# Moving the split tokens' rows by 128 bytes, and another first batch of idle matmuls

## The chip, the core and the metric

The kernel runs on one core of one Trainium2 chip. The metric is the device time of one execution in microseconds (us). Five engines work side by side, each through its own instruction queue in order: TensorE (PE in the profile; its weight loads are a row of their own, PEld), VectorE (DVE), ScalarE (ACT), GpSimd (POOL) and SyncE (SP). Here SP and POOL start nearly all transfers (DMA), and ACT starts the first five.

## The reference, cut to what matters

One layer of a decoder trunk is computed for 4096 prompt tokens and 64 sample tokens, all in float32:

```
h = rmsnorm(x) * norm_pre
z = h @ w_in                    # 1024 -> 2816 columns: the input projection
out_a = silu(g) * B * conv3(C * h_in)
out_b = silu(g) * window_attention(q, k, v, sinks)
out_c = silu(g) * cross_attention(q, memory)
y = concat(out_a, out_b, out_c) @ w_out
x = x + rmsnorm(y) * norm_post
```

The projection `z` is 22 column tiles of 128 for 4160 tokens; with `y` it is most of the arithmetic.

## The kernel before, in words

**How a product is made.** TensorE multiplies float32 at full speed only in the rounded type `float32r`. So each operand is split into a rounded part `hi` and a remainder `lo`, and a product is three matmuls: `hi` of the weights with `hi` of the tokens, `hi` with `lo`, and `lo` with `hi`. `product` (L360 to L368) does this for one weight tile of 512 rows by 128 columns and one tile of 260 tokens: 4 slices of 128 rows by 3 matmuls, 12 matmuls of 260 columns, all at L367. Each has its own weight load. The token rows (`hi`, `lo`) are the moving operand, which streams through the array; the weight slices are the stationary operand, which is loaded into it.

**The input projection.** Token blocks of 520 (two tiles of 260) and weight tiles in pairs go through Strassen-Winograd products (seven instead of eight); the first two blocks go through eight plain products. `PHASES` lists the pairs of column tiles in three phases. A phase's weights stay in SBUF while all eight blocks pass. Altogether L367 is executed 7488 times: 624 products of 12.

**Where the operands lie.** Tiles come from pools that are laid out one behind the other in every partition. The weight slots (`wa`, `wb`; 4096 bytes each) begin at byte 224 of a 256-byte period in both pools; a slice lies 512 bytes behind the one before it, so all weight slices begin at 224 modulo 256. `split` (L354) and `x_split` (L576) put `hi` and `lo` into slots of pool `hp`, tiles of 4 rows of 320 floats (1280 bytes, five periods; 260 floats are used). In the kernel before, `hp` begins so that every such row lies at 96 modulo 256: 128 bytes off the weights. These residues are read from the addresses in the built program.

**The output projection** (`Block.run`, L1491) swaps the roles: the weights of `w_out` (in slots of `wa`) are the moving operand with 512 columns, and the split rows `mh`, `ml` of 128 tokens (also in slots of `wa`) are the stationary one, so both lie at 224 modulo 256. One block is an exception: the 64 sample tokens' rows `mh_s` lie in another pool's tile at 96. The last block also has matmuls of 256 columns, from the same slots.

**The start.** POOL fills `ident`, `mhalf` and `ones`; ACT and SP load the first tokens and weights. Meanwhile TensorE runs nine idle matmuls (L701, `ones` times `ident`, float32, whose records are 18 of 128 columns), whose result is not used. The first products then wait for the first weights, split by ACT (L181) and DVE (L185).

**What sets the order.** The program up to the end of phase 0 is kept in the written order on all engines (`manual_schedule`, opened just ahead of the first loads); the rest is ordered by a scheduler. The change moves no instruction in it.

Of the kernel before, what the change touches and what calls it, by code (L numbers as in the profile page):

```python
# [8 lines left out]
F32 = mybir.dt.float32  # L9
F32R = mybir.dt.float32r  # L10
# [5 lines left out]
P = 128  # L16
D = 1024
KT = D // P
KH = KT // 2
# [5 lines left out]
XR = 320  # L25
# [22 lines left out]
def f(ap):  # L48
    return ap.bitcast(F32)
# [3 lines left out]
def hybrid_layer(ctx: ExitStack, tc: tile.TileContext, a: dict):  # L53
    nc = tc.nc
    TE, V, S, G, DMA = nc.tensor, nc.vector, nc.scalar, nc.gpsimd, nc.sync
# [7 lines left out]
    ident = const.tile([P, P], F32, name="ident")  # L63
# [21 lines left out]
    pa = ExitStack()  # L85
# [3 lines left out]

    place = ctx.enter_context(tc.tile_pool(name="place", bufs=1)).tile([P, 2, KH, HW], F32, name="place")  # L90
    hxp = pa.enter_context(tc.tile_pool(name="hx", bufs=4))
    hp = pa.enter_context(tc.tile_pool(name="hp", bufs=2))
    own = ExitStack()
    kept_z = ExitStack()
# [38 lines left out]
    def accumulator(i, w, name):  # L133

        tag = "xy"[i % 2]
        if pa1 is None:
            return pa2[tag].tile([P, 2, 512], F32, tag=tag, name=name)
        return pa1[tag, w].tile([P, w, 512], F32, tag="c", name=name)
# [367 lines left out]
    ones = own.enter_context(tc.tile_pool(name="ones", bufs=1)).tile([P, P], F32, name="ones")  # L506
# [69 lines left out]
    def x_split(b, o, meanwhile=lambda: None):  # L576
        x = xs[0, b][o]
        h0[b, o] = hi, lo = [hp.tile([P, KH, XR], F32R, tag=n, name=f"{n}0_{b}{o}")[:, :, :HW] for n in ("hi", "lo")]
        for k in range(KH):
            if k == 1:  # L580
                meanwhile()
            g = gain_of(o, k)
            S.mul(hi[:, k], x[:, k], g)
            V.scalar_tensor_tensor(lo[:, k], x[:, k], g, f(hi[:, k]), op0=ALU.mult, op1=ALU.subtract)
# [5 lines left out]
    def first_fill(o, q, raw=None):  # L590
        ws[0, q, o] = w_slot(q, f"w0_{q}{o}")
        w_split(ws[0, q, o], raw0.pop((q, o)) if raw is None else raw)
# [104 lines left out]
    x_of(0, 0, "B21")  # L697

    idle = accumulator(1, 2, "idle")
    for _ in range(9):  # L700
        TE.matmul(idle[:, 0, :P], ones, ident, start=True, stop=True)  # L701
    x_split(0, "B11", lambda: first_fill("A21", 0))
    for q in range(4):
        if q > 0:
# [977 lines left out]
```

## Time and profile before

| | us |
|---|---|
| median of 3 runs | 1545.25 |
| lowest and highest | 1545.03, 1546.0 |
| span of the profiled execution | 1545.6 |
| TensorE busy in it | 1535.3 |
| VectorE busy | 1145.3 |
| ScalarE busy | 805.6 |
| GpSimd busy | 378.5 |
| PE line L367 on the chain that ended last | 48.9% of the span |

The span runs from the first to the last instruction of one profiled execution; it is 0.35 us above the median of the runs. Times inside the execution are counted from the span's start. In rows of the timeline the columns are: start, time from the first start to the last end (us), engine, line, operation, output and inputs, size, count, and in brackets the engine's idle time just ahead and what ended it. Matmuls are pipelined: one of 260 columns is recorded with about 0.28 us, while the next one starts about 0.12 us after it. So the pace of a stretch is the time from one start to a later start, divided by the number of matmuls between them.

### The profile page before, as it was taken

The page shows a single profiled execution, that of the slowest core. Times are in us where ns is not written, and L with a number is a line of the kernel's source. Part 1 is how long each engine was busy: PE and PEld are TensorE (multiplying, and loading weights), DVE is VectorE, ACT ScalarE, POOL GpSimd, SP SyncE. Part 2 cuts the span into 40 slices and gives each one's busy share as a digit, 9 for nine tenths or more (in the row PEclk, how much of TensorE's full clock was granted, in tenths as well). Part 3 has the DMA queues.
Part 4 walks back from the last instruction along what each step waited for, and adds up shares of the span by engine and source line. Part 5 has one row for each costly group of instructions (what it writes and reads, how often), then busy time and mean ns, then how long its engine had stood idle before and what let it go on. Part 6 is the DMA issues. An engine that isn't in the chain of part 4 may idle for free.

```text
span 1545.6 us, 30168 instructions
## 1 busy us (share of the span) xinstructions
PE 1535.3 (99%) x11341; PEld 1413.2 (91%) x11341; DVE 1145.3 (74%) x2055; ACT 805.6 (52%) x2039; POOL 378.5 (24%) x603
## 2 busy tenths in 40 slices
PE   9999999999999999999999999999999999999998
PEld 9999999999999999999999998788888888887876
DVE  6779887898888777896777769766666666666643
ACT  6776665475322222344454447665556655655632
POOL 0223332211400000000100203544444444444310
PEclk9999999999999999999999999999999999999999
DMA  9879999778755333578777788987777677777432
GB/s 282 187 203 234 272 281 268 264 241 299 193 180 179 126 125 113 196 221 278 229 259 244 207 303 264 243 159 164 147 159 149 147 151 161 150 161 154 129 110 95
DMA packets 177942, 306.28 MB, mean 198 GB/s; under 512 B 33925, under 2 KB 107653, under 8 KB 177765
## 3 DMA queue, kind: packets, MB, share of 16 engines
q1 hardware_dynamic: 130901, 227.38, 47.4%
q0 software_dynamic: 46176, 75.92, 24.9%
q8 instruction: 90, 1.47, 0.4%
q10 hardware_dynamic: 720, 1.05, 0.2%
q14 instruction: 55, 0.45, 0.1%
HBM read 197.23 MB, written 108.05 MB: 198 GB/s over the span
## 4 chain that ended last, share of the span: by engine, by line
PE 87%; DMA 5%; DVE 4%; issue 2%; POOL 1%; ACT 1%; SPq 0%; ACTq 0%; DVEq 0%; POOLq 0%
PE c L367 49%; PE y L1491 22%; PE ws L1245 4%; PE wo L1087 2%; PE wt L1268 2%; PE xs L1181 2%; PE xt L1196 2%; PE wo L1217 2%; DMA md<-th 1%; PE wo L1223 1%; DVE z L374 1%; PE mem_acc L788 1%; DMA qd<-z 1%; DMA nat<-in_x_p 1%; DMA x_4B<-in_xt 1%
## 5 line engine op out<-in xcount | busy, mean ns | idle before, releaser
L1491 PE MATMUL y<-wo,mh 128*128 128x512 f32 (+1 forms) x1040 | 350.1, 399 | 0.0
L374 DVE TENSOR_TENSOR z<-c,z 128x520 f32<-128x520 f32 (+1 forms) x308 | 194.8, 646 | 90.1 <-PE c L367 89.0
L1491 PEld LDWEIGHTS y<-wo,mh 128*128 128x128 f32 x1040 | 194.3, 188 | 39.4 <-issue 2.4
L1491 PE MATMUL y<-wo,ml 128*128 128x512 f32 (+1 forms) x520 | 201.9, 388 | 0.0
L1258 ACT ACTIVATE sm<-sm,wnm 128x128 f32<-128x128 f32 x256 | 99.6, 391 | 60.8 <-DVE wnm L1252 60.0
L1190 POOL TENSOR_SCALAR xp<-xp,xrd 128x256 f32<-128x256 f32 x128 | 74.3, 588 | 208.1 <-DVE xrd L1186 208.1
L1491 PEld LDWEIGHTS y<-wo,ml 128*128 128x128 f32 x520 | 98.2, 189 | 16.2
L1182 DVE TENSOR_REDUCE xmx<-xs 128x2 f32<-128x512 f32 x64 | 44.1, 689 | 59.6 <-PE xs L1181 59.3
L1270 ACT COPY wpt<-wt 128x512 f32<-128x512 f32 x64 | 37.3, 582 | 86.8 <-PE wt L1268 84.3
L1245 PEld LDWEIGHTS ws<-kst,q 128*128 128x128 f32 x512 | 70.1, 190 | 5.4 <-ACT xp L1185 0.7
L1498 DVE TENSOR_TENSOR yn<-y,gpost 128x512 f32<-128x512 f32 (+1 forms) x66 | 45.1, 683 | 39.6 <-PE y L1491 39.3
L1245 PE MATMUL ws<-kst,q 128*128 128x256 f32 x512 | 73.1, 283 | 0.4 <-ACT xp L1185 0.4
L1499 ACT ACTIVATE y<-y 128x512 f32<-128x512 f32 (+1 forms) x66 | 38.6, 584 | 64.2 <-DVE yn L1498 64.2
L736 POOL CAST wmask<-negs 128x256 uint8<-128x256 f32 x1 | 1.1, 1076 | 270.9 <-DMA negs<-in_wmask 270.9
L1278 POOL TENSOR_SCALAR_AFFINE_SELECT wpt<-wpt 128x512 f32<-128x512 f32 x64 | 52.6, 821 | 42.7 <-ACT wpt L1270 39.8
L1185 ACT ACTIVATE xp<-xs,xnm 128x256 f32<-128x256 f32 x128 | 58.9, 464 | 7.1 <-DVE xnm L1183 7.1
L1120 POOL DMA_DIRECT2D q<-qd x64 | 42.8, 674 | 71.2 <-DVE wo L185 61.1
L1109 POOL DMA_DIRECT2D kst<-qd x64 | 38.7, 617 | 63.9 <-PE xt L1196 41.5
L1248 DVE COPY_PREDICATED sm<-wmask,ws 128x256 f32<-128x256 uint8 x124 | 52.2, 436 | 2.7 <-ACT sm L1247 2.3
L1509 DVE SCALAR_TENSOR_TENSOR xr<-yn,yst,xr 128x1024 f32<-128x1024 f32 (+2 forms) x34 | 43.1, 1269 | 14.2 <-POOL yst L1505 13.3
L376 ACT COPY z<-c 128x520 f32<-128x520 f32 (+1 forms) x44 | 24.3, 553 | 55.8 <-PE c L367 53.3
L1275 POOL TENSOR_SCALAR_AFFINE_SELECT wpv<-wpt 128x512 f32<-128x512 f32 x62 | 40.2, 648 | 50.8 <-ACT wpt L1270 50.7
(961 smaller groups left out, 5144.1 us busy)
## 6 DMA issues: line engine op xcount, KB each, us to landing
q<-qd POOLq DMA_DIRECT2D x64, 384.0 KB
xr<-in_x_p SPq DMA_DIRECT2D x32, 512.0 KB
nat<-in_x_p SPq DMA_DIRECT2D x39, 416.0 KB
o_yp<-xr SPq DMA_DIRECT2D x31, 512.0 KB
md<-th POOLq DMA_DIRECT2D x48, 260.0 KB
qd<-zh SPq DMA_DIRECT2D x48, 260.0 KB
qd<-z SPq DMA_DIRECT2D x48, 260.0 KB
kst<-qd POOLq DMA_DIRECT2D x60, 192.0 KB
```

Of the source, the lines that this page charges most:

```text
L367: TE.matmul(bank[:, :HW], l, r, start=first and i == 0, stop=last and i == 3 * KH - 1)
L374: add = lambda dst, other: V.tensor_tensor(dst, c, other, op=ALU.add)
L1182: V.tensor_reduce(mx[:, :nb], s, axis=AX.X, op=ALU.max)
L1185: S.activation(p[:, i, :], s[:, i, :], AF.Exp, bias=nm[:, i : i + 1], scale=SCALE, accum_out=den[:, i : i + 1])
L1190: G.tensor_scalar(p[:, i, :], p[:, i, :], rd[:, i : i + 1], 0.5, op0=ALU.mult, op1=ALU.mult)
L1245: TE.matmul(s3[:, hh, :], self.q[:, 4 + 2 * (2 * half + hh) + kvh, i * P : i * P + P], self.kst[:, 2 * kvh + part, i * P : i * P + 2 * P], ...
L1248: V.copy_predicated(sm[:, 2 * half : 2 * half + 2, :], third["wmask"], third["negs"] if first else s3[:, :, 0:P])
L1258: S.activation(sm[:, hh, :], sm[:, hh, :], AF.Exp, bias=nm[:, hh : hh + 1], scale=SCALE, accum_out=den[:, hh : hh + 1])
L1278: G.affine_select(p3, p3, pattern=[[0, 4], [1, P]], compare_op=ALU.is_ge, fill=0.0, base=0, channel_multiplier=-1)
L1491: TE.matmul(acc, self.hl[l][:, k], wo[k][c0 // 512][:, r, c0 % 512 : c0 % 512 + c1 - c0], start=j == 0, stop=j == passes * KT - 1)
L1498: V.tensor_tensor(yn[:m, c0:c1], acc[:m], gpost[:m, c0:c1], op=ALU.mult)
L1509: V.scalar_tensor_tensor(self.xr[:m, cs], yn[:m, cs], st[:m, 3:4], self.xr[:m, cs], op0=ALU.mult, op1=ALU.add)
```

## The change

A pool `shift` of 32 floats (128 bytes) is put between the pools `hx` and `hp`, and never written or read. It moves `hp`, and the pools laid out behind it for the projection (row factors, temporaries, `z` tiles), by 128 bytes. Every row of `hi` and `lo` then lies at 224 modulo 256, like the weights. The pools of the output projection and the attention keep their addresses, since they are opened anew once the projection's pools are closed.

The nine idle matmuls of 128 columns give way to fourteen of 260 to 512 columns (5488 in all), on a tile of ones in the rounded type, which takes a slot of `hp` and is filled by POOL.

```
+    pa.enter_context(tc.tile_pool(name="shift", bufs=1)).tile([P, 32], F32, name="shift")
     hp = pa.enter_context(tc.tile_pool(name="hp", bufs=2))
...
     idle = accumulator(1, 2, "idle")
-    for _ in range(9):
-        TE.matmul(idle[:, 0, :P], ones, ident, start=True, stop=True)
+    warm = hp.tile([P, KH, XR], F32R, tag="lo", name="warm").rearrange("p k n -> p (k n)")
+    G.memset(f(warm[:, : P + 512]), 1.0)
+    for n in (416, 416, 416, 416, 512, 512, 512, 416, 416, 416, 260, 260, 260, 260):
+        TE.matmul(idle[:, 0, :n], warm[:, :P], warm[:, P : P + n], start=True, stop=True)
```

Three lines more stand ahead of the rest, so L367 becomes L368 and L701 becomes L704.

The first rows of TensorE's queue at the start of the program, before (`idle` is the unused result, `c` an accumulator of the projection, `hi`, `lo` the split tokens, `w` the split weights):

```order
L701 MATMUL idle<-ident,ones 128x128 x9
L367 MATMUL c_0_0_0_267<-hi_0B_229,w_0A_233 128x260
L367 MATMUL c_0_0_0_267<-lo_0B_230,w_0A_233 128x260
L367 MATMUL c_0_0_0_267<-hi_0B_229,w_0A_233 128x260 x2
L367 MATMUL c_0_0_0_267<-lo_0B_230,w_0A_233 128x260
```

And now:

```order
L704 MATMUL idle<-warm 128x416 x4
L704 MATMUL idle<-warm 128x512 x3
L704 MATMUL idle<-warm 128x416 x3
L704 MATMUL idle<-warm 128x260 x4
L368 MATMUL c_0_0_0_278<-hi_0B_240,w_0A_244 128x260
L368 MATMUL c_0_0_0_278<-lo_0B_241,w_0A_244 128x260
```

Only the idle matmuls differ; what follows keeps its order to the end of the program.

GpSimd's queue at the same place, before (`r` are row factors, made much later):

```order
masks.py:197 MEMSET ident 128x128
L66 MEMSET mhalf 128x8
L507 MEMSET ones 128x128
masks.py:199 ISA
masks.py:199 AFFINE_SELECT ident<-ident 128x128
L281 TENSOR_SCALAR r_497<-r_497 104x5
```

And now:

```order
masks.py:197 MEMSET ident 128x128
L66 MEMSET mhalf 128x8
L508 MEMSET ones 128x128
masks.py:199 ISA
masks.py:199 AFFINE_SELECT ident<-ident 128x128
L702 MEMSET warm 128x640
L282 TENSOR_SCALAR r_508<-r_508 104x5
```

One memset is added, and the first idle matmul waits for it instead of for `ident`.

## The prediction

> **What bounds the kernel now.** I read the page first: its span, and the chain of work that ended last by engine and by line.
>
> ```profile
> span 1545.6 us, 30168 instructions
> ...
> PE 87%; DMA 5%; DVE 4%; issue 2%; POOL 1%; ACT 1%; SPq 0%; ACTq 0%; DVEq 0%; POOLq 0%
> PE c L367 49%; PE y L1491 22%; PE ws L1245 4%; PE wo L1087 2%; PE wt L1268 2%; PE xs L1181 2%; PE xt L1196 2%; PE wo L1217 2%; DMA md<-th 1%; PE wo L1223 1%; DVE z L374 1%; PE mem_acc L788 1%; DMA qd<-z 1%; DMA nat<-in_x_p 1%; DMA x_4B<-in_xt 1%
> ```
>
> TensorE is on 87% of the chain, L367 alone on 49%. A busy PE isn't a PE at its peak, so the next question is how fast its matmuls follow each other. The view of the chain in order of time gives long unbroken pieces of L367 with their counts (start, length, engine, line, matmuls):
>
> ```profile
> 9.39 49.44 PE c L367 x406
> ...
> 86.51 68.18 PE c L367 x564
> 160.67 9.23 DMA x_4B<-in_xt
> ...
> 241.75 113.64 PE c L367 x936
> ...
> 486.56 229.77 PE c L367 x1895
> ...
> 799.47 4.32 PE c L367 x36
> 804.23 4.36 PE c L367 x36
> ```
>
> And the busy times in three stretches without a gap (PE busy, number of matmuls, clock, DMA share, GB/s):
>
> ```profile
> 120.00:210.00 90.00, 90.00 (x752) 1.00 1.00 269
> 245.00:355.00 110.00, 110.00 (x911) 1.00 0.83 259
> 490.00:710.00 220.00, 220.00 (x1819) 1.00 0.50 168
> ```
>
> Two or three of each count began ahead of the stretch. So 90 us hold 750 matmuls, 120.0 ns each; 110 us hold 908 and 220 us hold 1817, 121.1 ns each. The same instructions, at the same clock, keep one of **two paces**, 120.0 or 121.1 ns, for hundreds of microseconds. The short pieces show it too: 4.32 us / 36 = 120.0 and 4.36 / 36 = 121.1. Nothing waits there, so something inside a matmul and its weight load sets the pace, and operand addresses are a candidate.
>
> Does an address matter at all? The kernel holds one comparison. In the output projection the operands agree modulo 256; only the 64 sample tokens' block, `mh_s`, has them 128 bytes apart. Timeline of TensorE, first a stretch of agreeing operands, then the two ends of the `mh_s` block, and that tile's own row (shortest, median, longest record):
>
> ```profile
> 1530.29 0.39 PE L1491 MATMUL y<-wo,ml 128*128 128x512 f32 x1
> 1530.51 0.62 PE L1491 MATMUL y<-wo,mh 128*128 128x512 f32 x2
> 1530.97 0.39 PE L1491 MATMUL y<-wo,ml 128*128 128x512 f32 x1
> ```
>
> ```profile
> 1520.57 1.79 PE L1491 MATMUL y<-wo,mh_s 128*128 128x512 f32 x7
> ...
> 1528.02 0.39 PE L1491 MATMUL y<-wo,mh 128*128 128x512 f32 x1
> ```
>
> ```profile
> L1491 PE MATMUL y<-wo,mh_s x32: 390/392/404, 1520.6 to 1527.8; 128*128 128x512 f32 x32
> ```
>
> From 1530.29 to 1530.97 lie three starts: 0.68 us / 3 = 226.7 ns. From 1520.57 to 1528.02 lie 32: 7.45 / 32 = 232.8 ns. Apart costs 6.1 ns a matmul here. (That block also uses each weight slice twice running, so it isn't a pure comparison.) The other row I need is that of the last block's 256 columns, operands agreeing:
>
> ```profile
> 1537.89 0.28 PE L1491 MATMUL y<-wo,ml 128*128 128x256 f32 x1
> 1538.01 0.40 PE L1491 MATMUL y<-wo,mh 128*128 128x256 f32 x2
> 1538.25 0.28 PE L1491 MATMUL y<-wo,ml 128*128 128x256 f32 x1
> ```
>
> Three starts in 0.36 us: 120.0 ns, with four columns fewer than L367 has.
>
> **The change part by part. First, the shift.** It adds no instruction; it changes the residue of 7488 moving operands from 96 to 224, that of the weights. No row of before shows 260 columns with agreeing operands, so I bound the new pace. From below: 256 columns, agreeing, run steadily at 120.0, and I see no reason why more columns should go faster; so not under 120.0. From above: agreeing operands took 120.0 ns at 256 columns and 226.7 at 512, which is 0.417 ns a column plus 13.3; the same line gives 121.67 ns at 260. A further bound, by the 6.1 ns above in full, would be 120.6 - 6.1 = 114.5; it contradicts the first one. I take **120.0 throughout**: L367 itself already keeps 120.0 for long stretches at 260 columns, so four columns more fit into that time, and where operands agree the trace shows each size settle on one even pace.
>
> What that saves is what the slow pace costs now. A long piece on the chain ends with its last record, 0.16 us after the time at which the next matmul could start. So 49.44 - 0.16 - 406 x 0.120 = 0.56 us; 68.18 - 0.16 - 564 x 0.120 = 0.34; 113.64 - 0.16 - 936 x 0.120 = 1.16; 229.77 - 0.16 - 1895 x 0.120 = 2.21; and in the third phase about 14 groups of 36 at 4.36 instead of 4.32, 0.56. Sum 4.8 us. In between the chain leaves TensorE: the row at 160.67 is the first long transfer on it. But PE already runs at 120.0 there (the stretch from 120 to 210), so nothing is to be gained. Work that is late next is what could eat some of the 4.8: in the two long pieces PE alone is on the chain for 344 us, so 3.4 of it looks safe, and of the rest I let 0.4 be lost in waits for transfers. That leaves **4.4 us**.
>
> The shift also moves the landing places of transfers (`z` and temporaries, by 128 bytes). The temporaries already lie at many residues, 32 bytes apart from slot to slot, with transfers no row of which stands out. I cost it at nothing; where DMA is full (share 1.00 from 120 to 210) a slower landing would show first.
>
> **Second, the idle matmuls.** How the start goes now: a memset of POOL, the idle matmuls, a piece of TensorE's timeline, and the chain of the first 12 us.
>
> ```profile
> 0.99 0.20 POOL L507 MEMSET ones<- 128x128 f32 x1
> ```
>
> ```profile
> 1.58 4.21 PE L701 MATMUL idle<-ident,ones 128*128 128x128 f32 x18 [1.58 <-POOL ident masks.py:199]
> ```
>
> ```profile
> 7.01 0.42 PE L367 MATMUL c<-lo_0B,w_0A 128*128 128x260 f32 x1
> 7.23 0.51 PE L367 MATMUL c<-hi_0B,w_0A 128*128 128x260 f32 x2
> 7.58 0.28 PE L367 MATMUL c<-lo_0B,w_0A 128*128 128x260 f32 x1
> 7.70 0.40 PE L367 MATMUL c<-hi_0B,w_0A 128*128 128x260 f32 x2
> ```
>
> ```profile
> 1.75 6.21 DMA wr_1A<-in_w_in
> ...
> 8.64 0.70 DVE w_1A L185
> ...
> 9.39 2.69 PE c L367 x20
> ```
>
> The array starts slow: 0.22 us a matmul of 260 columns at 7.01, 0.12 from 7.58 on; the pace changes at about 7.4. The chain up to 9.39 is the transfer of the second weight tile, its rounding on ACT (in the lines left out) and its remainder on DVE; PE's own pace is hidden behind it. New: a memset of 640 columns. 128 columns take 0.20 us; `ident` is ready at 1.58, so at five times that it ends by 1.58 + 1.0 = 2.6, or earlier if part of the 0.20 is a fixed share. I take 2.3 for the first idle matmul. All 5488 columns at the slow pace are 5488 x 0.22 / 260 = 4.6 us, so they end by 6.9; at the full pace they would take about half. The first product starts where the old ones' records end, at about 1.58 + 4.21 = 5.8, so it comes up to 1.1 us later. It and the two matmuls behind it (14 x 0.12 = 1.7 us at full pace, 3.1 at the slow one) must be done by 9.39: from 6.9 they end at 8.6 if the array is at full pace by then, and at 10.0 if it is slow all along, 0.6 late. With the change of pace at 7.4, as now, they end at 8.9. So I take **0**, with bounds 0 and +1.0 (0.6, and a few slow matmuls more behind 9.39). Nothing below zero, since the transfer isn't touched. `warm` takes a slot of `lo` that DVE fills again only for the second token tile, long after.
>
> **Sum:** 1545.6 - 4.4 = 1541.2 against the profiled span; that execution lies 0.35 above the median of the runs, so 1540.9.
>
> **The rivals.**
>
> *Nothing changes (22%).* The two paces may have nothing to do with the residue: 232.8 against 226.7 may come from the repeated weights, and the pace may be set by where a stall leaves the two streams. Then both paces stay, in other places: 1544 to 1547. The Trainium skill speaks for this one, in "TensorE: Matmul & The Clock Gate", Part 2, step 1: TensorE has two independent read ports into SBUF, and loading the next weights takes no bandwidth from the running matmul. By that rule no shift could matter. The 6.1 ns speak against it, as far as that block is comparable.
>
> *Slower (18%).* Agreeing operands may keep the line of 0.417 ns a column plus 13.3. At 260 columns that is 121.67 ns against a mean of 120.6 now (the 4.8 us over 7488 matmuls are 0.6 ns above 120.0): 7488 x 1.07 = 8.0 us, 1553.3. For it: both agreeing sizes lie on it. Against it: 260 columns have been seen at 120.0, so 13.3 isn't a floor for the gap. It decides as soon as the settled pace of agreeing operands at 260 columns lies above 120.6. In the same direction, an even worse lock (6%): 1560 and more.
>
> *Much faster (9%).* The 6.1 ns come off in full: 7488 x 6.1 = 46 us, about 1500. The 120.0 of 256 agreeing columns speaks against it.
>
> **How the numbers follow.** Forecast 45%, its own range 1539.5 to 1543. With 22, 18, 6 and 9% for the others, a range that leaves out no more than 2 in 10 has to take in the slower line and can leave out the two far cases: 1536 to 1554. About 0.2% (3.1 us, below 1542.2 or above 1548.3) is what a measurement of this kernel can tell from no change. Faster by more than that: 40 of the 45, the 9, and 2 of the 22, 51%. Slower: 18 and 6 and 2, 26%. Within: 23%.
>
> **What will show it.** Right: stretches such as 245 to 355 and 490 to 710 hold a number of matmuls that gives 120.0, pieces of 36 on the chain are all 4.32, and the piece at 9.39 still follows the DVE remainder of the second weight tile. Wrong: if 4.36 pieces stay, the residue doesn't choose the pace; if L367 settles at 121.67 or any value above 120.6, the line holds; if below 120.0, the weights and the moving rows did collide all the time. If the first piece starts after 9.39 with PE itself ahead of it on the chain, the idle matmuls are too long.

## The result and the profile after

| kernel | median us | runs | lowest to highest | ratio to before, 95% interval |
|---|---|---|---|---|
| before | 1545.62 | 4 | 1545.03 to 1549.8 | |
| after | 1535.09 | 4 | 1533.46 to 1537.75 | 0.9927 [0.9905, 0.9949] |

The change gains 0.73%, 11 us (8 to 15 by the interval), more than twice the 4.4 us of the forecast, and the time lies just below the range. The profiled execution took 1533.46 us with a span of 1531.7, against 1545.6 before: 13.9 us less. This pair of profiles shows more than the medians do. The execution is the fastest of the four, and a time lies about 1.8 us above its span, so the one profiled before took about 1547.4 us (an estimate from its span), more than the median of before. The page of the changed kernel (span, busy time by engine, then the chain of work that ended last by engine and by line; L368 is the old L367):

```profile
span 1531.7 us, 30162 instructions
...
PE 1520.7 (99%) x11337; PEld 1398.8 (91%) x11337; DVE 1145.3 (75%) x2055; ACT 806.1 (53%) x2039; POOL 380.0 (25%) x604
...
PE 93%; DVE 3%; DMA 1%; ACT 1%; issue 1%; POOL 0%; SPq 0%; DVEq 0%; POOLq 0%; ACTq 0%
PE c L368 53%; PE y L1494 23%; PE ws L1248 4%; PE wo L1090 2%; PE wt L1271 2%; PE xs L1184 2%; PE xt L1199 2%; PE wo L1220 2%; PE wo L1226 1%; PE mem_acc L791 1%; DMA nat<-in_x_p 1%; DMA ws18A<-in_w_in 0%; DMA ws20A<-in_w_in 0%; DVE x_2T L348 0%; PE idle L704 0%
```

TensorE holds more of the chain than before (93% against 87%), and the span is shorter all the same. It was busy for 1520.7 us, 14.6 less than the 1535.3 of before, while its idle time went from 10.3 to 11.0. So it isn't waits that went; its matmuls follow each other faster. The chain in order of time, from the idle matmuls to the pieces of L368 that the prediction read (start, length, engine, line, matmuls):

```profile
2.16 4.37 PE idle L704 x14
6.53 50.52 PE c L368 x420
...
112.51 236.80 PE c L368 x1992
...
479.46 225.15 PE c L368 x1895
...
706.00 4.32 PE c L368 x36
711.69 4.27 PE c L368 x36
...
876.57 52.04 PE c L368 x432
```

The piece of 1895 took 229.77 us before. Less the 0.16 us of its last record, that was 229.61 / 1895 = 121.2 ns a matmul; now it is 224.99 / 1895 = **118.7 ns**. The piece of 1992 has 236.64 / 1992 = 118.8. Pieces of 36 come as 4.32 (120.0) and as 4.27 (118.6), none in the chain as 4.36. The last long piece keeps a slower pace, 51.88 / 432 = 120.1. Two stretches of TensorE by themselves (PE busy, matmuls, clock, DMA share, GB/s):

```profile
120.00:210.00 90.00, 90.00 (x761) 1.00 1.00 276
...
490.00:710.00 220.00, 220.00 (x1850) 1.00 0.53 178
```

They held 752 and 1819 before. The clock is full in both kernels, and the DMA share in the first stretch is 1.00 in both. Over all starts of that line that follow the one before without a wait and within 0.2 us, the mean distance fell from 120.6 to 118.8 ns: 1.8 ns x 7488 = 13.5 us.

The start, TensorE's timeline from the idle matmuls to the second product:

```profile
2.16 4.37 PE L704 MATMUL idle<-warm 128*128 128x416 f32 x14 [2.16 <-POOL warm L702]
6.36 0.28 PE L368 MATMUL c<-hi_0B,w_0A 128*128 128x260 f32 x1
6.49 0.28 PE L368 MATMUL c<-lo_0B,w_0A 128*128 128x260 f32 x1
...
8.01 0.28 PE L368 MATMUL c<-hi_0B,w_1A 128*128 128x260 f32 x1
...
8.27 0.51 PE L368 MATMUL c<-hi_0B,w_1A 128*128 128x260 f32 x2
```

The idle matmuls start at 2.16 and the first product at 6.36. Eight of its twelve distances are 0.12 us, from the first on, and the other four 0.15 to 0.23; before, they were 0.22 to 0.38 until about 7.4. The third matmul of the second product starts at 8.27, 1.1 us ahead of the 9.39 of before. The transfer landed sooner in this execution: ACT begins to round the second weight tile at 6.82, where it began at 7.99 before and at 8.34 in a later execution of the same changed kernel (e10). So about 1.1 us of the 13.9 belong to this execution's start and not to the pace.

### The profile page after: what moved, and what is told of

It reads as the page before. It is cut to its first block, busy times and chain, and to the rows that moved or that the text cites. A ratio compares the mean times of both kernels' runs of the same rounds, so it can differ in the third digit from the quotient of the medians.

```text
span 1531.7 us, 30162 instructions
## 1 busy us (share of the span) xinstructions
PE 1520.7 (99%) x11337; PEld 1398.8 (91%) x11337; DVE 1145.3 (75%) x2055; ACT 806.1 (53%) x2039; POOL 380.0 (25%) x604
## 4 chain that ended last, share of the span: by engine, by line
PE 93%; DVE 3%; DMA 1%; ACT 1%; issue 1%; POOL 0%; SPq 0%; DVEq 0%; POOLq 0%; ACTq 0%
PE c L368 53%; PE y L1494 23%; PE ws L1248 4%; PE wo L1090 2%; PE wt L1271 2%; PE xs L1184 2%; PE xt L1199 2%; PE wo L1220 2%; PE wo L1226 1%; PE mem_acc L791 1%; DMA nat<-in_x_p 1%; DMA ws18A<-in_w_in 0%; DMA ws20A<-in_w_in 0%; DVE x_2T L348 0%; PE idle L704 0%
## 5 line engine op out<-in xcount | busy, mean ns | idle before, releaser
L1512 DVE SCALAR_TENSOR_TENSOR xr<-yn,yst,xr 128x1024 f32<-128x1024 f32 (+2 forms) x34 | 43.1, 1269 | 14.0 <-POOL yst L1508 13.3
```

The costliest lines, as they stand in the source:

```text
L1512: V.scalar_tensor_tensor(self.xr[:m, cs], yn[:m, cs], st[:m, 3:4], self.xr[:m, cs], op0=ALU.mult, op1=ALU.add)
```

## The experiments

Three theories stood at the start. **A**: the distance between the moving rows and the weights, modulo 256 bytes, sets the pace. **B**: the way in which the array is entered from the idle matmuls does. **C**: the split tokens' own address does, or any other place of it would do. The runs of before beside the first four had a median of 1547.46 us (23 runs, 1541.99 to 1551.32), beside the next ones 1547.31 (23) and beside the last two 1545.69 (9), so ratios are compared, not times.

| run | distance of L368's operands | median us | ratio to before, 95% interval | span of the profile | the piece x1895 |
|---|---|---|---|---|---|
| e1_after_again | 0 | 1535.49 | 0.9937 [0.9916, 0.9957] | 1532.2 | 225.14 |
| e2_shift_only | 0 | 1537.42 | 0.9942 [0.9922, 0.9962] | 1531.2 | 225.14 |
| e3_idle_only | 128 | 1546.94 | 1.0002 [0.9990, 1.0015] | 1541.5 | 227.66 |
| e4_left_moved | 128 and 0 | 1542.05 | 0.9979 [0.9964, 0.9994] | 1540.0 | 227.32 |
| e5_shift256 | 128 | 1547.51 | 1.0004 [0.9992, 1.0015] | 1546.7 | 229.19 |
| e6_shift64 | 192 | 1543.99 | 0.9984 [0.9971, 0.9997] | 1542.4 | 227.67 |
| e9_keys192 | 0 | 1538.62 | 0.9955 [0.9941, 0.9968] | 1539.1 | |
| e10_after_beside | 0 | 1537.58 | 0.9938 [0.9924, 0.9951] | 1536.4 | 227.67 |

**Which part of the change does it.** The changed kernel again, then each of its two parts alone.

> The changed kernel once more, beside the others on one chip. All theories: 1533.5 to 1537.8 us, a mean of about 118.8 ns from one L368 matmul to the next.

```diff
--- after
+++ shift_only
-    warm = hp.tile([P, KH, XR], F32R, tag="lo", name="warm").rearrange("p k n -> p (k n)")
-    G.memset(f(warm[:, : P + 512]), 1.0)
-    for n in (416, 416, 416, 416, 512, 512, 512, 416, 416, 416, 260, 260, 260, 260):
-        TE.matmul(idle[:, 0, :n], warm[:, :P], warm[:, P : P + n], start=True, stop=True)
+    for _ in range(9):
+        TE.matmul(idle[:, 0, :P], ones, ident, start=True, stop=True)
```

> The shift with the old nine idle matmuls. A (the distance modulo 256 between the moving rows and the weights sets the pace): within 2 us of the changed kernel, 118.8 ns for the split tokens' matmuls. B (the entry from the idle matmuls sets the pace in which the streams lock): as before, 1545 us and 120.6 ns.

```diff
--- after
+++ idle_only
-    pa.enter_context(tc.tile_pool(name="shift", bufs=1)).tile([P, 32], F32, name="shift")
```

> The new idle matmuls without the shift. A: 1545 us within 1.5, paces of 120.0 and 121.1 ns as before. B: 1533 to 1538 us, 118.8 ns. Either way the start is seen by itself: the first product begins at about 6.4 us instead of 5.7.

The shift alone gives 0.9942, all of the changed kernel's 0.9937 within the intervals; the idle matmuls alone give 1.0002. B falls. The chain of the kernel with the idle matmuls alone shows their price at the start:

```profile
1.75 6.18 DMA wr_1A<-in_w_in
9.35 48.99 PE c L367 x406
...
484.60 227.66 PE c L367 x1895
```

The first long piece begins at 9.35, behind the same transfer, where it began at 9.39 before: nothing lost, nothing won. The last row holds a miss: 227.5 / 1895 = 120.05 where I expected this piece to be as slow as before. Distance 128 therefore has both paces, and which one a long piece takes differs between executions.

**Distance or place.** In the next kernel the 128 bytes lie ahead of the weights of quarters 0 to 2, so that the split tokens keep the address that the change gave them while the weights of those quarters move off by 128 again; those of the fourth, `w_3`, are at distance 0 in the first two phases.

```diff
--- after
+++ left_moved
+    ctx.enter_context(tc.tile_pool(name="shift", bufs=1)).tile([P, 32], F32, name="shift")
     wa = ctx.enter_context(tc.tile_pool(name="wa", bufs=3 * NP_))
...
-    pa.enter_context(tc.tile_pool(name="shift", bufs=1)).tile([P, 32], F32, name="shift")
```

> The 128 bytes are put ahead of the weights of quarters 0 to 2 and of the split tokens both, so that the split tokens lie where they do in the changed kernel, w_0 to w_2 lie 128 bytes off them (6120 matmuls) and w_3 in the first two phases lies at their distance 0 (1368 matmuls). A (distance): products with w_0 to w_2 at 120.0 to 121.1 ns, those with w_3 at 118.7, and 1541 to 1544 us, since a fifth or so of the gain stays. C (the split tokens' own address counts, whatever the weights'): all at 118.7, 1533 to 1538 us. None of the two: as before, 1545 us, with w_3 as slow as the rest.

This one execution has both distances side by side. Its timeline of TensorE, the first matmul of each of six products in a row (the eleven behind each are left out):

```profile
227.03 0.28 PE L368 MATMUL c<-hi_5B,w_3A 128*128 128x260 f32 x1
...
228.45 0.28 PE L368 MATMUL c<-hi_5B,w_0A 128*128 128x260 f32 x1
...
229.90 0.28 PE L368 MATMUL c<-hi_5B,w_1A 128*128 128x260 f32 x1
...
231.34 0.28 PE L368 MATMUL c<-hi_5B,w_2A 128*128 128x260 f32 x1
...
232.78 0.28 PE L368 MATMUL c<-hi_5B,w_3A 128*128 128x260 f32 x1
...
234.20 0.28 PE L368 MATMUL c<-hi_5T,w_0S 128*128 128x260 f32 x1
```

From start to start: 1.42, 1.45, 1.44, 1.44 and 1.42 us for twelve matmuls, 118.3 ns with `w_3` and 120 to 121 with the others (the rows are rounded to 0.01 us; over the whole trace the means are 118.8 and 120.2; before, `w_3` had the 120.6 of the others). The same rows of the same token tile run fast or slow with the weights that they meet. C falls for the tokens' own address. The time, 0.9979, is A's as well: about a third of the gain, from 18% of the matmuls at distance 0 and from others that stayed at 120.0 rather than 121.1.

The other form of C, that any other place would do, is tried by shifts of other sizes:

```diff
--- after
+++ shift256
-    pa.enter_context(tc.tile_pool(name="shift", bufs=1)).tile([P, 32], F32, name="shift")
+    pa.enter_context(tc.tile_pool(name="shift", bufs=1)).tile([P, 64], F32, name="shift")
```

> The shift is 256 bytes instead of 128: all addresses behind it move, but the distance modulo 256 is that of before. A (distance modulo 256): 1545 us within 1.5, paces of 120.0 and 121.1. C (any other place would do): 1533 to 1538 us and 118.8 ns.

```diff
--- after
+++ shift64
-    pa.enter_context(tc.tile_pool(name="shift", bufs=1)).tile([P, 32], F32, name="shift")
+    pa.enter_context(tc.tile_pool(name="shift", bufs=1)).tile([P, 16], F32, name="shift")
```

> The shift is 64 bytes: the distance is 192 (or 64 the other way) modulo 256. If only exact agreement helps: as before, 1545 us. If the two streams collide in a part of the rows that grows with how near to 128 they are: between, 1538 to 1543 us. If what counts is only not to be at 128: 1533 to 1538 us.

256 bytes give 1.0004: every address moved, the distance didn't, nothing gained. 64 bytes give 0.9984, a gain of 2.5 us (0.5 to 4.5). That is between the first two of the three cases named ahead and fits neither as it was put: agreement isn't needed for some gain, and the gain isn't graded by nearness to 128, as the paces further down show. Their chains, first of the 256 bytes, then of the 64:

```profile
86.45 269.24 PE c L368 x2221
```

```profile
115.00 239.32 PE c L368 x1992
...
485.24 227.67 PE c L368 x1895
```

269.08 / 2221 = 121.2 ns, the slow pace of before. At 64 bytes 239.16 / 1992 = 120.06 and 227.51 / 1895 = 120.06: this distance keeps 120.0 in its long pieces. That is the kernel which my forecast described, 120.0 throughout; it isn't the one that the change made.

**The paces by themselves.** Two kernels leave out the layer and run L368's pattern of twelve by itself, 192 matmuls for each size and distance, twice, the second time in the reverse order. In the loop, cut to what matters, `n` is the number of columns and `d` the distance in bytes; `w` holds four weight tiles, and `M` the moving rows, which begin at the weights' residue modulo 256.

```python
o = d // 4
for r in range(16):
    t, i = w[r % 4], 0
    for k in range(4):
        ks = slice(k * P, k * P + P)
        hi, lo = M[:, o + 320 * k : o + 320 * k + n], M[:, 2560 + o + 320 * k : 2560 + o + 320 * k + n]
        for l, x in ((t[:, 0, ks], hi), (t[:, 0, ks], lo), (t[:, 1, ks], hi)):
            TE.matmul(acc[:, :n], l, x, start=i == 0, stop=i == 11)
            i += 1
```

> Leaves out the whole computation: it only runs matmuls in the kernel's order of twelve (hi and lo rows with w_A, hi with w_B, four k tiles), 192 for each size and distance, twice, in two orders. A: at 260 columns distance 0 (and 256) gives about 118.7 ns and 128 gives 120.0 to 121.1; at 256 columns distance 0 gives 120.0 if the 120.0 of the kernel's last block belongs to the size, and less (about 117) if it belongs to that block; at 512 columns distance 128 costs up to 6 ns over distance 0. If the repeated weights of the mh_s block were its cost: 512 columns with each slice twice running are slower than without at both distances. If distance doesn't matter by itself: no difference over 0.5 ns at any size.

> Leaves out the whole computation, as the first such run: matmuls in the kernel's order of twelve at finer distances, and with both operands moved by 128 bytes together. If the distance alone sets the pace (A): the moved pairs repeat the unmoved ones, 260 columns at 118.7, 120.0 and 120.0 to 121.1 ns for distances 0, 64 and 128, 256 columns at 120.0, 118.7 and 113.4 for 0, 128 and 192. If the weights' own address has a part: other numbers. For distances under 32 bytes either 118.7 as at 0 (rows are fetched in pieces of 32 bytes or more) or 120.0 as at 32.

TensorE's timeline of the first of them: 256 columns at distances 0, 64, 128 and 192, 260 columns at 0, 32, 64, 96, 128 and 160, then 512 columns at 0, 64, 128 and 192 and, in the last two segments of 128 matmuls, at 0 and 128 with each weight slice used twice running:

```profile
135.50 23.19 PE L89 MATMUL ancrp<-m,w 128*128 128x256 f32 x192
158.53 22.78 PE L89 MATMUL ancrr<-m,w 128*128 128x256 f32 x192
181.15 22.94 PE L89 MATMUL ancrt<-m,w 128*128 128x256 f32 x192
203.93 21.95 PE L89 MATMUL ancrv<-m,w 128*128 128x256 f32 x192
225.71 22.95 PE L89 MATMUL andrp<-m,w 128*128 128x260 f32 x192
248.50 23.20 PE L89 MATMUL andrq<-m,w 128*128 128x260 f32 x192
271.54 23.20 PE L89 MATMUL andrr<-m,w 128*128 128x260 f32 x192
294.57 23.21 PE L89 MATMUL andrs<-m,w 128*128 128x260 f32 x192
317.62 23.41 PE L89 MATMUL andrt<-m,w 128*128 128x260 f32 x192
340.87 23.20 PE L89 MATMUL andru<-m,w 128*128 128x260 f32 x192
...
701.79 43.71 PE L89 MATMUL anjrp<-m,w 128*128 128x512 f32 x192
745.33 44.13 PE L89 MATMUL anjrr<-m,w 128*128 128x512 f32 x192
789.30 44.79 PE L89 MATMUL anjrt<-m,w 128*128 128x512 f32 x192
833.92 44.97 PE L89 MATMUL anjrv<-m,w 128*128 128x512 f32 x192
878.73 29.20 PE L89 MATMUL anjxp<-m,w 128*128 128x512 f32 x128
907.76 30.02 PE L89 MATMUL anjxt<-m,w 128*128 128x512 f32 x128
```

A pace is the difference of two starts over 192: 256 columns at distance 0 have (158.53 - 135.50) / 192 = **119.9 ns**, 260 columns at distance 0 have (248.50 - 225.71) / 192 = **118.7**. More columns do go faster. All paces, forward and reverse order where they differ by over 0.5 ns:

| columns | distance 0 | 64 | 128 | 192 |
|---|---|---|---|---|
| 248 | 113.3 / 115.0 | | 115.6 | |
| 252 | 116.7 | | 117.1 | |
| 256 | 120.0 | 117.8 | 118.7 | 113.4 |
| 260 | 118.7 | 120.0 | 121.1 / 120.0 | 120.0 |
| 264 | 121.3 / 120.0 | | 120.0 | |
| 272 | 125.4 | | 126.6 | |
| 288 | 131.7 | | 133.4 | |
| 320 | 146.6 | | 146.7 | |
| 384 | 173.3 | | 175.8 | |
| 512 | 226.8 | 229.0 | 232.4 | 233.4 |

260 columns at 32, 96, 160 and 224 also have 120.0, and at 256 again 118.7. With the weights used twice running, 512 columns have 226.8 at distance 0 ((907.76 - 878.73) / 128) and 233.3 at 128. So the 6.1 ns of the `mh_s` block belonged to the distance and not to its repeated weights.

In the second such kernel the pairs moved together repeat the paces (260 columns 118.7, 120.0, 120.0 / 121.1; 256 columns 120.0, 118.7, 113.4): the distance decides, not the address. Under 32 bytes the distances 4, 8 and 16 have the 120.0 of 32 (4 took 123.3 in the repeat); 24, and others near 128 and 256, have paces of their own. Timeline, 260 columns at distances 16, 24, 120, 128, 240, 248 and 252:

```profile
117.30 23.20 PE L89 MATMUL andrs<-m,w 128*128 128x260 f32 x192
140.33 23.84 PE L89 MATMUL andrt<-m,w 128*128 128x260 f32 x192
164.01 24.46 PE L89 MATMUL andru<-m,w 128*128 128x260 f32 x192
188.31 23.21 PE L89 MATMUL andrv<-m,w 128*128 128x260 f32 x192
211.35 22.95 PE L89 MATMUL andrw<-m,w 128*128 128x260 f32 x192
234.14 23.69 PE L89 MATMUL andrx<-m,w 128*128 128x260 f32 x192
257.67 23.20 PE L89 MATMUL andry<-m,w 128*128 128x260 f32 x192
```

120.0 at 16, (164.01 - 140.33) / 192 = 123.3 at 24, 126.6 at 120, 120.0 at 128, 118.7 at 240, 122.6 at 248. No distance tried beats 118.7 at 260 columns. Some pairs came out otherwise in this second kernel: 256 columns at 192 took 117.8 once and 113.5 once, at 64 likewise 117.8 and 113.4, and 512 columns at 128 took 233.3 instead of 232.4. A distance allows certain paces; which of them is kept isn't fixed by the distance.

**Can the rest of the kernel use it?** The window's keys are 256 columns at distance 0 (512 matmuls), the pair that is 120.0 where 113.4 was seen.

```diff
--- after
+++ keys192
-            self.kst = self.pool("k").tile([P, 4, P + CT], F32R, tag="k", name=f"kst{c}")
+            kst = self.pool("k").tile([P, 4 * (P + CT) + 64], F32R, tag="k", name=f"kst{c}")
+            self.kst = kst[:, 48 : 48 + 4 * (P + CT)].rearrange("p (j n) -> p j n", j=4)
```

> The changed kernel with the window's keys (256 columns, 512 matmuls of L1249) moved from distance 0 to distance 192 of their queries. By the pace that 256 columns showed by themselves, 120.0 at 0 and 113.4 at 192, they fall from 120.4 to about 113.8 ns: 512 x 6.6 = 3.4 us of span where TensorE is the bound, 1532 us if the changed kernel beside it has 1535.5. If the keys' matmuls are limited otherwise there (by their weights, which each serve two of them, or by waits): no change, 1535.5.

> The changed kernel beside the one with the keys moved: 1535.5 us, L1248 at 120.4 ns.

No gain that the times show: 0.9955 against 0.9938 beside it, the intervals overlap. One group of the keys and what starts behind it, with the keys moved and then in the changed kernel:

```profile
1007.83 1.11 PE L1249 MATMUL ws<-kst,q 128*128 128x256 f32 x8
1008.78 0.38 PE L1200 MATMUL xt<-ident,xp 128*128 128x128 f32 x2
```

```profile
1004.68 1.11 PE L1248 MATMUL ws<-kst,q 128*128 128x256 f32 x8
1005.63 0.38 PE L1199 MATMUL xt<-ident,xp 128*128 128x128 f32 x2
```

0.95 us for eight, 118.8 ns, in both. Over the 59 groups of eight that run without a wait the mean is 118.2 with the keys moved and 119.3 beside it: 1.1 ns of the 6.6 that I expected, 0.6 us in all. The keys run in groups of eight between other matmuls, and such a group doesn't show the pace that 192 in a row have. (They also use each weight slice twice; which of the two keeps them from 113.4 wasn't separated.) So no version here beats the changed kernel.

The second execution of the changed kernel says something else. Its span is 1536.4, 4.2 us over that of e1, and its chain has the piece

```profile
481.77 227.67 PE c L368 x1895
```

where e1 has 225.14: 120.06 ns instead of 118.7, with the same program. At distance 0 the line has two paces too, 118.7 and 120.0. In e1 about 40 products (of twelve) without a wait kept 120.0 and 550 the fast pace, in e10 about 270 and 320; 230 products x 12 x 1.3 ns = 3.6 us, the larger part of the 4.2.

## Why the prediction was right and wrong

**The step that failed** is the lower bound of the shift's pace: "256 columns, agreeing, run steadily at 120.0, and I see no reason why more columns should go faster; so not under 120.0". By themselves 256 agreeing columns have 120.0 and 260 have 118.7. The pace isn't a rising function of the columns at a given distance: it falls from 256 to 260, and 256 columns alone range from 113.4 to 120.0 with the distance. The 120.0 of the last block was an unlucky pair of size and distance, not a floor. The forecast took away only the difference between the two old paces (4.8 us); the shift took both down, to 118.7 for most products and 120.0 for the rest, and the mean fell by 1.8 ns where I had 0.6.

**What held, and what was luck.** The distance between the operands does set the pace (e2, e4, e5, e7), as the forecast had it. The sign that led there doesn't prove it. Two paces stand at one and the same distance, before (120.0 and 121.1 at 128) as after (118.7 and 120.0 at 0), so their number says nothing of the addresses; and e10 is against "where operands agree the trace shows each size settle on one even pace". That the guess was right is in part luck. The better sign was `mh_s`: its 6.1 ns were an effect of the distance at 512 columns. They don't carry over to 260, where distance 0 is worth 1.3 to 2.4.

The idle matmuls at nothing: e3 shows it, 1.0002 with an interval of 0.9990 to 1.0015. Their working came out close: first one at 2.16 (taken 2.3), first product at 6.36 (up to 6.9). That they hide behind the transfer of the second weight tile holds in e3 (9.35), but not in the profile of the changed kernel: there the transfer came sooner, and the chain runs through the idle matmuls themselves. The 0.4 us set aside for waits compare with 0.7 us more idle time of TensorE.

**The rivals.** *Nothing changes* fell: e1 and e5, which differ only in the size of the pad, lie 0.7% apart, and 512 columns differ by up to 6.6 ns with the distance alone. The prediction had put behind this rival a rule of the Trainium skill ("TensorE: Matmul & The Clock Gate", Part 2, step 1: two independent read ports, so that loading the next weights takes no bandwidth from the running matmul). These measurements are against the rule as the prediction used it, that no shift could matter; what the ports themselves do no run shows. *Slower by the line* fell as well: 0.417 ns a column plus 13.3 gives 133.3 at 288 and 126.7 at 272, measured 131.7 and 125.4; it holds from 320 up, and 260 agreeing columns lie 3 ns under it. *Much faster* carried the effect of 512 columns over to 260. The true outcome lay between the forecast and this last rival, in a gap that the failed bound had closed. Of the signs named ahead, "pieces of 36 all 4.32" belongs to e6, the kernel at 120.0; the changed one shows 4.27, and with it the sign that was given for the case below 120.0.

**What stays open.** That the two reads, of moving rows and of weights, get in each other's way is the reading that fits a dependence on their distance alone; no run saw the collision itself. Nor was it found what chooses between the two paces of a distance: it differs between executions, and no run controlled it. It changes mostly behind breaks: the profiles of before and after hold 27 unbroken runs of 70 matmuls and more (each start under 0.135 us behind the one before), up to 1968 long, and none of them changed its pace on the way. In e2 one run of 816 went from 120.0 to 118.7 after its first 144.

## What to carry to other kernels

Where thousands of matmuls follow each other without a wait, look at the distance modulo 256 between moving rows and weights, and measure it with a loop of the kernel's own pattern at the exact size: a neighbouring size or another block gives no bound. Two paces in one kernel are no sign of a bad distance, since the good one has two as well. A change of alignment costs no instruction, but the long unbroken runs profited most; groups of eight won 1.1 ns of 6.6. Compare several executions, since one program can keep different paces from run to run.

## What the runs showed of the hardware that was not expected

At one granted clock of 1.00, 260 columns took 118.7 to 126.6 ns and 256 columns 113.4 to 120.0, with nothing changed but the distance of their operands, and the distances that are good at one size are not those of another: at 256 columns 0 is the worst of the four (120.0 each time) and 192 the best in the first of the two kernels, at 512 it is the other way round. Nor do more columns always take longer: at distance 0, 256 took 120.0 ns and 260 took 118.7. One distance can have two steady paces (118.7 and 120.0 at 0, 120.0 and 121.1 at 128), kept for up to 1968 matmuls in a row; that made about 3.6 of the 4.2 us between two executions of the same changed kernel. At 256 columns and distances 64 and 192 two paces, 113.4 and 117.8, were seen as well.
